# The output projection of an attention layer: prepared weights, one written order, and the seven products in another sequence

## The chip, the cores and the metric

The kernel runs on one core of a Trainium2 chip. A core has TensorE (PE: matmuls; PEld is its weight load), VectorE (DVE), ScalarE (ACT), GpSimd (POOL) and SyncE (SP), which here only issues DMAs. The engines run side by side, each through its own list of instructions in order. The metric is the device time of one execution in microseconds (us); lower is better.

## The reference

One model forward in float32 over 1024 latent tokens of width 1024 and 256 context tokens: an attention layer (windowed, 16 heads of 128), then a convolution layer (width 2048), each with a gate path, and a final norm. The part that the change touches is the end of the attention layer:

```
o = windowed_attention(q, k, v, kc, vc, sink)      # (1024, 2048)
y = (o * silu(z)) @ w_out                          # w_out: (2048, 1024)
x = x + gate * y
# then the next layer: rmsnorm(x), modulated, into the convolution's input projection
```

## The kernel before

**Precision.** Each matmul operand is held as a high part (rounded to the matmul's format, made by a copy on ACT) and a low part (the rest, made by a subtraction, `split_lo`, on DVE or POOL). A product takes three matmuls: high·high, high·low, low·high.

**Stages.** After a prologue, attention runs in 128 steps (8 pairs of heads, 16 blocks of 64 tokens): scores, softmax, transposes, values, with the input projection's matmuls filled in between. Then comes the output projection (`proj_attn`), then the convolution layer (`b_mm` for its input projection, then its own output projection).

**The output projection in seven products.** A = o·silu(z) is stored in DRAM, transposed, as `ozd`. It is cut in halves by tokens (h) and by its 2048 rows of K, W = `w_out` in halves by K and by columns (m), and the four quarters of the result are made with seven half-size products instead of eight. Two products, A11·W11 and A12·W21, are the steps with r = 0 of the list `SEQA` (eight steps); the other five have r = 1 to 5 and take sums of quarters. A step is 256 rows of K: four blocks b of 128 tokens, six matmuls of 512 columns each, so 24 matmuls. Steps 0 to 6 have their blocks 0 and 1 done inside attention (`EARLY_ROWS`), the remaining blocks follow after it.

**Weights prepared in attention.** The generator `low_parts` runs a little with each attention step. It makes the four sums of quarters of W that the products take (POOL, `minus`) and stores them in `wsums`, then the low parts of W's first 512 columns (`wolA`) and of the second layer's output weights (`wolC`). Each low part is one ACT copy and one POOL subtraction of 128x512 elements; `after` keeps them behind the softmax's operations of the same step. `store()` sends results out one step later.

**Operands of a step.** `load` fetches tiles of `ozd` and weights, `split` combines tiles on DVE and makes high and low parts; for r ≥ 1 the weights' low parts come from POOL. `ahead(nl, ns)` says up to which step loads and splits have been written. Loads go by SP's queue.

**Results.** Partial products are kept in SBUF (`m1`, `u2`, `u4`) and added on DVE from PSUM; `joined` multiplies such a partial result by the gate and adds it to the residual, on POOL; `evac0` then takes the last product from PSUM, multiplies by the gate, adds, stores x and squares it on ACT. It normalizes each 128-token block as soon as it is there (eight chains of norms of one column each). `turn_in` transposes normalized rows for the next layer (4 transposes a tile; DVE, ACT, then DVE or POOL); `bgA` places these tiles behind the steps, two at a time. The last three steps (`BYBLOCK`) are run block by block, not step by step.

**Order.** The program is written once for all engines. A planner reorders it by times that it models, except where `pin` keeps an engine in written order (`InOrder`, `keep_in_program_order`). From the end of the prologue only PE is pinned.

Of the kernel before, what the change touches and what calls it, by code (L numbers as in the profile page):

```python
# [40 lines left out]
LOAD_TO = {0: (8, 7), 1: (8, 7), 2: (9, 7), 4: (9, 8), 5: (10, 8), 6: (10, 8), 7: (11, 9)}  # L41
# [56 lines left out]
def backbone_kernel(  # L98
# [619 lines left out]
    wolA, wolC = (dr.tile([m, NK, P, 2, 512], F32, tag=n, name=n) for n, m in (("wolA", 1), ("wolC", 2)))  # L718
    wsums = dr.tile([4, NK // 2, P, 2, 512], F32, tag="wsums", name="wsums")
# [5 lines left out]
    made = []  # L725
# [8 lines left out]
    def low_parts():  # L734

        def raw(ap, name):
            t = pg.alloc(F32, [2, 512], name)
            SY.dma_start(out=t, in_=ap)
            return t

        def minus(a, b, at):
            after(tt(G, at, a, b, ALU.subtract), anchor_p)

        def pair(kt):
            return raw(Wo[kt * P:kt * P + P].rearrange("p (m n) -> p m n", m=2), "wb")

        def keep(t, which, kt):
            for m in range(2):
                made.append((wsums[which[m], kt // 2][:, kt % 2], t[:, m], t if m == 0 else None))

        u = pair(0)
        yield "open"
        for kt in range(KT):
            store()
            t = pair(kt + KT)
            minus(u[:, 1], u[:, 0], u[:, 0])
            yield "open"
            minus(t[:, 1], u[:, 1], u[:, 1])
            yield "open"
            minus(t[:, 1], u[:, 0], t[:, 1])  # L760
            keep(u, (0, 2), kt)
            yield "open"
            store()
            if kt + 1 < KT:
                u = pair(kt + 1)
            minus(t[:, 0], t[:, 1], t[:, 0])
            keep(t, (3, 1), kt)
            yield "shut"
        store()
        items = [(pair_rows(w, m, kk), d[m, kk]) for w, d, n in ((Wo, wolA, 1), (Wp, wolC, 2)) for m in range(n)  # L770
                 for kk in range(NK)]
        his = pg.alloc(F32R, [2, 512], "lhi")
        for src, dst in items:
            t = raw(src, "low")
            store()
            yield "open"
            for b in range(2):
                after(act(his[:, b], t[:, b], AF.Copy), anchor_a)
                after(split_lo(G, t[:, b], t[:, b], his[:, b]), anchor_p)
                if b == 0:  # L780
                    yield "open"
            made.append((dst, t, t))
            yield "shut"
        store()
        pg.free(his)
# [6 lines left out]
    def proj_attn():  # L792
# [14 lines left out]
        def load(i):  # L807
            r, kk = SEQA[i]
            if r == 0:
# [3 lines left out]
            k2 = kk + NK // 2  # L813
            rows = {1: ((1, kk), (1, k2), (0, kk)), 2: (), 3: ((0, k2),), 4: ((0, kk), (1, kk)), 5: ((1, k2),)}[r]
            st[i] = [o_raw(*a) for a in rows] + [w_raw(pair_rows(Wo, 1, k2) if r == 3 else
                                                       wsums[{1: 1, 2: 0, 4: 2, 5: 3}[r], kk])]
# [20 lines left out]
        def split(i):  # L837
# [3 lines left out]
            *rows, w = st[i]  # L841
            keep = False
            if r == 1:
                a21, a22, f = rows
                tt(V, a21, a21, a22, ALU.add)
                pg.free(a22)
                tt(V, f, a21, f, ALU.subtract)
                kept[(1, kk)], kept[(2, kk)] = a21, f
                keep = True
            elif r == 2:  # L850
                f = kept.pop((1, kk))
# [5 lines left out]
            elif r == 4:  # L857
                f, a21 = rows
                tt(V, f, f, a21, ALU.subtract)
                pg.free(a21)  # L860
            else:
                f, = rows
            oh, wh = pg.alloc(F32R, [2, 512], "ozh"), pg.alloc(F32R, [2, 512], "woh")
            act(wh, w, AF.Copy)
            act(oh, f, AF.Copy)
            wl, ol = pg.alloc(F32R, [2, 512], "wol"), pg.alloc(F32R, [2, 512], "ozl")
            for e in range(2):
                split_lo(G, wl[:, e], w[:, e], wh[:, e])
            split_lo(V, ol, f, oh)
            pg.free(w)  # L870
            if not keep:
# [25 lines left out]
        m1, u2, u4 = [], [], []  # L897

        def half_pages(ts, b, name):
            if b % 2 == 0:  # L900
                ts.append(pg.alloc(F32, [2, 512], name))
            return ts[b // 2][:, b % 2]
# [7 lines left out]
        for i in range(EARLY_ROWS):  # L910
            ahead(min(i + EA, EARLY_ROWS - 1), min(i + 1, EARLY_ROWS - 1))
            for b in range(2):
                yield from block(i, b, banks[4 + b])
                if i == 3:
                    act(half_pages(m1, b, "m1"), banks[4 + b], AF.Copy)
# [12 lines left out]
        def joined(us, xrs, m, keep=False):  # L928
            ns = slice(m * 512, m * 512 + 512)
            for b in range(4):  # L930
                u = us[b // 2][:, b % 2]
                g = hp.alloc(F32, None, "ug")
                tt(G, g[:, 0:512], u, gbc0[0][:, ns], ALU.mult)
                for xr in xrs:
                    t = xr[b // 2][:, b % 2]
                    tt(G, t, t, g[:, 0:512], ALU.add)
                hp.free(g)
                if b % 2 and not keep:
                    pg.free(us[b // 2])
# [3 lines left out]
        acc = [banks[b] for b in (4, 5, 0, 1)]  # L943
        for i, b in order:
            if b == 2 and i != 3:
                ahead(*LOAD_TO[i])
            if i == 4 and b == 2:
                xr = residual(0, 0)
            run(block(i, b, acc[b]))
            if i == 3:  # L950
                act(half_pages(m1, b, "m1"), acc[b], AF.Copy)
            if b == 3:
                done(i)
                bgA(0, i)
                if i == 4:
                    joined(m1, [xr], 0, True)
        for b in range(4):
            evac0(0, 0, b, acc[b], xr)
        held = []
        for i in range(8, len(SEQA)):  # L960
            r, kk = SEQA[i]
            acc = [banks[b] for b in ((2, 3, 4, 5) if r < 4 else (0, 1, 2, 3))]
            ahead(i + 3, i)
            if (r, kk) == (2, 2):
                xr12, xr22 = residual(0, 1), residual(1, 1)
            if (r, kk) == (3, 1):
                joined(u4, [xr12, xr22], 1)
            if (r, kk) == (4, 2):
                xr = residual(1, 0)
            if i >= len(SEQA) - BYBLOCK:  # L970
                ahead(i + 3, i + 1)
                held.append(i)
                bgA(r, kk)
                if kk == 3:
                    for b in range(4):
                        for n in held:
                            run(block(n, b, acc[b]))
                        evac0(1, 0, b, acc[b], xr)
# [3 lines left out]
            for b in range(4):  # L982
                run(block(i, b, acc[b]))
                if kk == 3 and r in (1, 2, 4):
                    with tc.high_priority():
                        d = {1: u2, 2: u4, 4: u2}[r]
                        d = half_pages(d, b, "u") if r < 4 else d[b // 2][:, b % 2]
                        tt(V, d, acc[b], (m1 if r == 1 else u2)[b // 2][:, b % 2], ALU.add)
                if b == 2:
                    ahead(i + 3, i + 1)  # L990
            done(i)
            bgA(r, kk)
            if kk == 3 and r > 2:
                for b in range(4):
                    evac0(r - 3, 1, b, acc[b], xr12 if r == 3 else xr22)
            if (r, kk) == (1, 3):
                pg.free(*m1)
            if (r, kk) == (4, 3):
                joined(u2, [xr], 0)
# [3 lines left out]
    def evac0(h, m, b, acc, xr):  # L1003
# [3 lines left out]
        if b % 2 == 0:  # L1007
            x1[(m, b // 2)] = pg.alloc(F32, [2, 512], "x1")
        if first:
            x1[b] = small([P, 2], name="ssf", bufs=8)  # L1010
        t, ss = x1[(m, b // 2)][:, b % 2], x1[b]
        tt(V, t, acc, gbc0[0][:, ns], ALU.mult)
        tt(G if b % 2 and h == 0 and first else V, t, t, xr[b // 2][:, b % 2], ALU.add)
# [4 lines left out]
        act(junk[:, 0:512], t, AF.Square, accum_out=ss[:, 1 - first:2 - first])  # L1018
        hp.free(junk)
        if first:  # L1020
            V.tensor_scalar(out=ss[:, 0:1], in0=ss[:, 0:1], scalar1=1.0 / D, scalar2=EPS, op0=ALU.mult, op1=ALU.add)
            return
        r = rstd_of(ss[:, 1:2], D, 1, ss[:, 0:1])
        for m in range(2):
            if b % 2 == 0:
                x1[("n", m, b // 2)] = pg.alloc(F32, [2, 512], "xn")
            d, f = x1[("n", m, b // 2)][:, b % 2], x1[(m, b // 2)][:, b % 2]
            if m:
                act(d, f, AF.Copy, scale=r)
            else:  # L1030
                V.tensor_scalar(out=d, in0=f, scalar1=r, scalar2=None, op0=ALU.mult)
            if b % 2:
                pg.free(x1[(m, b // 2)])
        if b == 3:
            h2pg[h] = []
            for kt in range(KT):
                later.append(lambda h=h, kt=kt: turn_in(h, kt))
# [420 lines left out]
    for i, (pr, st) in enumerate(steps):  # L1458
# [36 lines left out]
        if lstate[0] == "open" or i >= 5 and (h % 4 < 3 or qb < LOWS):  # L1495
            lstate[0] = next(lows, "shut")
        else:
# [541 lines left out]
    def bgA(r, kk):  # L2039
# [105 lines left out]
```

## Time and profile before

| | |
|---|---|
| median of 3 runs | 1703.49 us (1703.44 to 1707.1) |
| profiled execution | 1705.04 us, its span 1703.3 us |
| PE busy | 1657.2 us (97%) |
| DVE, ACT, POOL busy | 1155.3, 876.3, 1002.7 us |
| DMA | 248.85 MB, mean 146 GB/s |
| projection after attention | 805.3 to 989.4 us in the span |

The span runs from the first instruction to the last; the execution's own time is 1.7 us longer. In the profile, names are those of the program with numbers left out: `woh`, `wol` are high and low parts of weights, `wo` a loaded weight tile, `ozf` a loaded tile of `ozd`, `ozh`, `ozl` its parts, `m`, `u`, `x`, `xr`, `xn` partial results, output rows, residual and normalized rows, `hf`, `h2h`, `h2l` the next layer's input. `pss`, `psg`, `pso` are PSUM banks. Nearly all instructions carry line 92, a helper, so groups are told apart by tiles. A row "PE pss <- ACT m_page: 11.0, 2, 9.8" says that PE waited for ACT's work on that tile 11.0 us in total, 2 times, 9.8 us the longest.

### The profile page before, as it was taken

The page shows a single profiled execution, that of the slowest core. Times are in us where ns is not written, and L with a number is a line of the kernel's source. Part 1 is how long each engine was busy: PE and PEld are TensorE (multiplying, and loading weights), DVE is VectorE, ACT ScalarE, POOL GpSimd, SP SyncE. Part 2 cuts the span into 40 slices and gives each one's busy share as a digit, 9 for nine tenths or more (in the row PEclk, how much of TensorE's full clock was granted, in tenths as well). Part 3 has the DMA queues.
Part 4 walks back from the last instruction along what each step waited for, and adds up shares of the span by engine and source line. Part 5 has one row for each costly group of instructions (what it writes and reads, how often), then busy time and mean ns, then how long its engine had stood idle before and what let it go on. Part 6 is the DMA issues. An engine that isn't in the chain of part 4 may idle for free. (4 is left out here: it accounts for less than half of the span.)

```text
span 1703.3 us, 23865 instructions
## 1 busy us (share of the span) xinstructions
PE 1657.2 (97%) x8244; PEld 1385.0 (81%) x8244; DVE 1155.3 (68%) x2099; ACT 876.3 (51%) x1527; POOL 1002.7 (59%) x911
## 2 busy tenths in 40 slices
PE   9999999999999999999799699999999999999998
PEld 6888888888888888888577578888888888888886
DVE  5755554555355544565657979999999999867832
ACT  5644443555355544555343465655665665466731
POOL 0247673666547573742659857999898888130300
PEclk9999999999999999999799899999999999999999
DMA  9436553454335443467776222010121202377981
GB/s 383 162 94 191 171 167 112 140 167 126 104 116 175 133 143 91 144 229 257 258 236 204 99 81 100 13 63 25 49 75 38 93 32 80 124 260 246 326 285 51
DMA packets 142042, 248.85 MB, mean 146 GB/s; under 512 B 45034, under 2 KB 61730, under 8 KB 141920
## 3 DMA queue, kind: packets, MB, share of 16 engines
q1 hardware_dynamic: 135840, 237.35, 42.0%
q10 hardware_dynamic: 6080, 9.97, 2.4%
q8 instruction: 65, 1.06, 0.3%
q14 instruction: 57, 0.47, 0.1%
HBM read 190.90 MB, written 45.88 MB: 139 GB/s over the span
## 5 line engine op out<-in xcount | busy, mean ns | idle before, releaser
L92 POOL TENSOR_TENSOR odd_half<-odd_half,prod_half 128x513 f32<-128x513 f32 (+2 forms) x252 | 314.1, 1254 | 22.9 <-ACT prod_half L92 9.6
L92 POOL TENSOR_TENSOR wlo_page<-wraw_page,whi_page 128x512 fp32r<-128x512 f32 (+1 forms) x104 | 174.3, 1690 | 130.9 <-ACT whi_page L92 123.7
L92 PE MATMUL psg<-hh_page,whi_page 128*128 128x512 f32 x600 | 237.1, 395 | 0.0
L92 PE MATMUL psg<-hl_page,whi_page 128*128 128x512 f32 x600 | 235.0, 392 | 0.0
L92 PE MATMUL psg<-hh_page,wlo_page 128*128 128x512 f32 x600 | 234.5, 391 | 0.0
L92 ACT ACTIVATE prod_half<-ubuf,dww 128x513 f32<-128x513 f32 (+2 forms) x252 | 165.7, 675 | 116.8 <-POOL odd_half L92 113.1
L92 PE MATMUL psg<-h2h_page,whi_page 128*128 128x512 f32 x464 | 182.1, 392 | 0.0
L92 PE MATMUL psg<-h2h_page,wlo_page 128*128 128x512 f32 x464 | 180.9, 390 | 0.0
L92 PE MATMUL psg<-h2l_page,whi_page 128*128 128x512 f32 x464 | 180.8, 390 | 0.0
L92 DVE SCALAR_TENSOR_TENSOR pss<-ubuf,dww,pss 128x512 f32<-128x512 f32 (+3 forms) x270 | 172.7, 672 | 0.1
L92 DVE SCALAR_TENSOR_TENSOR pss<-ubuf,wsum,pss 128x512 f32<-128x512 f32 (+3 forms) x270 | 172.0, 672 | 0.2
L92 POOL TENSOR_SCALAR p_page<-p_page,sc 128x576 f32<-128x576 f32 (+2 forms) x128 | 93.2, 728 | 112.2 <-DVE sc L92 106.8
L92 ACT ACTIVATE pt<-pss 128x640 fp32r<-128x640 f32 (+1 forms) x128 | 86.6, 676 | 132.7 <-PE pss L92 132.5
L92 ACT ACTIVATE p_page<-p_page,sc 128x577 f32<-128x577 f32 (+2 forms) x128 | 96.9, 757 | 86.9 <-DVE sc L92 86.3
L92 DVE CUSTOM_DVE_ANT_0 p_page<-pss,mask_page,nsink 128x576 f32<-128x576 f32 (+1 forms) x112 | 90.2, 805 | 74.5 <-PE pss L92 48.5
L92 PEld LDWEIGHTS psg<-hh_page,wlo_page 128*128 128x128 f32 x600 | 112.8, 188 | 24.1
L92 PEld LDWEIGHTS psg<-hh_page,whi_page 128*128 128x128 f32 x600 | 112.8, 188 | 19.6 <-ACT hh_page L92 0.3
L92 PEld LDWEIGHTS psg<-hl_page,whi_page 128*128 128x128 f32 x600 | 113.2, 189 | 19.0 <-DVE hl_page L92 0.2
L92 DVE TENSOR_TENSOR pt<-pss,pt 128x640 fp32r<-128x640 f32 (+1 forms) x128 | 100.7, 787 | 32.2 <-ACT pt L92 32.1
L92 PE MATMUL pso<-h2h_page,wlo_page 128*128 128x512 f32 x304 | 118.4, 390 | 0.0
L92 PE MATMUL pso<-h2h_page,whi_page 128*128 128x512 f32 x304 | 118.4, 389 | 0.0
L92 PE MATMUL pso<-h2l_page,whi_page 128*128 128x512 f32 x304 | 118.4, 389 | 0.0
(273 smaller groups left out, 4060.4 us busy)
## 6 DMA issues: line engine op xcount, KB each, us to landing
wraw_page<-in_k_wconv_dram SPq DMA_DIRECT2D x48, 512.0 KB, 3.2
wraw_page<-in_k_win_dram SPq DMA_DIRECT2D x40, 512.0 KB, 4.0
ozf_page<-ozd SPq DMA_DIRECT2D x36, 512.0 KB, 5.5
wo_page<-in_conv_w_out_dram SPq DMA_DIRECT2D x32, 512.0 KB, 5.6
wol_page<-wolC SPq DMA_DIRECT2D x32, 512.0 KB, 5.6
rope_half<-rope_half ACTq DMA_DIRECT2D x76, 128.0 KB, 2.5
araw_page<-in_k_ada_dram SPq DMA_DIRECT2D x16, 512.0 KB, 10.0
dww_raw<-in_ada_w_dram SPq DMA_DIRECT2D x64, 128.0 KB, 2.7
```

Source lines behind the costliest of these rows:

```text
L92: r = f(*a, **k)
```

## The change

1. *Weights.* `low_parts` also makes the low parts of three of the four sums (`wslow`, 24 of 128x512) and of the lower half of W's second 512 columns (8 more in `wolA`): 32 more ACT copies and POOL subtractions in attention. High and low parts now go through half pages (`hp`, six of them, shared with the rotary embedding), and each half is stored at once. One more piece is run in twelve of the attention's steps, and loads pause near a change of head group.
2. *Order.* DVE, ACT and POOL are pinned beside PE for the rest of `proj_attn`, that is all of it after attention. SP's queue is left to the planner.
3. *Products.* S1·T1 comes before S2·T2 (S1 = A21 + A22, S2 = S1 − A11, T1, T2 sums of W). Fewer tiles of `ozd` are loaded (20 instead of 28 for r ≥ 1), three of the five products load low parts of sums and one those of a plain quarter, so POOL makes them only for r = 1. PSUM banks rotate over all six. Splits are written two steps ahead, loads three (`AHEAD`), with other values of `LOAD_TO` for the first product.
4. *Results.* `joined` is gone. DVE adds the kept partial sums to the last product (`first_sum`) as each block ends; gate, residual, store and squares (`evac0`) are written after the next step's loads and splits, from SBUF; the norm of a half is made once for its four blocks (`norm0`). `turn_in` tiles of the first half start one step earlier, behind r = 4, kk = 1.

```diff
-LOAD_TO = {0: (8, 7), 1: (8, 7), 2: (9, 7), 4: (9, 8), 5: (10, 8), 6: (10, 8), 7: (11, 9)}
+LOAD_TO = {4: (9, 7), 5: (9, 7), 6: (9, 8), 7: (10, 9)}
+AHEAD = (3, 2)
...
+        def low(t, b, d):
+            h = hp.alloc(F32R, None, "lhi")
+            hv = h[:, 0:512]
+            after(act(hv, t[:, b], AF.Copy), anchor_a)
+            after(split_lo(G, hv.bitcast(F32), t[:, b], hv), anchor_p)
+            SY.dma_start(out=d, in_=hv.bitcast(F32))
+            hp.free(h)
...
+            low(u, 1, wslow[2, kt // 2][:, kt % 2])
...
+            low(t, 1, wslow[1, kt // 2][:, kt % 2])
+            yield "open"
+            low(t, 0, wslow[3, kt // 2][:, kt % 2])
...
-            rows = {1: ((1, kk), (1, k2), (0, kk)), 2: (), 3: ((0, k2),), 4: ((0, kk), (1, kk)), 5: ((1, k2),)}[r]
...
+            rows = {1: ((1, kk), (1, k2)), 2: ((0, kk),), 3: ((0, k2),), 4: (), 5: ((1, k2),)}[r]
+            n = (0, 0, 1, None, 2, 3)[r]
+            st[i] = [[o_raw(*a) for a in rows], w_raw(pair_rows(Wo, 1, k2) if r == 3 else wsums[n, kk]),
+                     None if r == 1 else w_raw(wolA[1, k2] if r == 3 else wslow[n, kk], F32R)]
...
+                a21, f = rows
+                tt(V, f, a21, f, ALU.add)
+                kept[(1, kk)], kept[(3, kk)] = f, a21
             elif r == 2:
+                f, = rows
+                s1, a21 = kept.pop((1, kk)), kept[(3, kk)]
+                tt(V, a21, f, a21, ALU.subtract)
+                tt(V, f, s1, f, ALU.subtract)
...
+            acc = [banks[(2 + 4 * (r - 1) + b) % 6] for b in range(4)]
+            ahead(i + AHEAD[0], i + AHEAD[1])
+            while finish:
+                h, m, xr = finish.pop()
+                for b in range(4):
+                    evac0(h, m, b, xr)
+                norm0(h, m)
...
+                m, v = part("m", b), part("v", b)
+                if r == 1:
+                    tt(V, v, acc[b], m, ALU.add)
+                elif r == 2:
+                    tt(V, v, acc[b], v, ALU.add)
+                    tt(V, m, acc[b], m, ALU.add)
+                else:
+                    first_sum(r - 3, 1, b, acc[b], v)
+                    if r == 4:
+                        tt(V, m, acc[b], m, ALU.add)
...
+    def first_sum(h, m, b, acc, u):
+        if b % 2 == 0:
+            x1[(m, b // 2)] = pg.alloc(F32, [2, 512], "x1")
+        tt(V, x1[(m, b // 2)][:, b % 2], acc, u, ALU.add)
...
-        for _ in range(2 if r == 0 and kk or r == 4 and kk >= 2 or r == 5 and kk < 2 else 0):
+        for _ in range(2 if r == 0 and kk or r == 4 and kk or r == 5 and kk < 2 else 0):
...
+    pin("PVAG")
     run(projA)
+    pin("P")
```

More of the change, by code (lines that the diff above doesn't have):

```diff
@@ L914, in proj_attn @@
                 if i == 3:
[L915 removed]
+                    act(part("m", b), banks[4 + b], AF.Copy)
         yield "early"
@@ L954, in proj_attn @@
                 bgA(0, i)
[L955 to L958, printed above, removed]
         held = []
+        finish = [(0, 0, xr)]
         for i in range(8, len(SEQA)):
             r, kk = SEQA[i]
[L962 to L969, printed above, removed]
+            acc = [banks[(2 + 4 * (r - 1) + b) % 6] for b in range(4)]
[5 more added lines that the diff above has]
+                norm0(h, m)
+            if kk == 1 and r in (3, 4, 5):
+                xr = residual(*{3: (0, 1), 4: (1, 1), 5: (1, 0)}[r])
             if i >= len(SEQA) - BYBLOCK:
-                ahead(i + 3, i + 1)
                 held.append(i)
@@ L1006, in evac0 @@
         rows = slice((4 * h + b) * P, (4 * h + b + 1) * P)
[L1007 to L1013, printed above, removed]
+        if first and b == 0:
+            x1["ss"] = [small([P, 4], name="ssx4", bufs=2) for _ in range(2)]
+        t, ss = x1[(m, b // 2)][:, b % 2], x1["ss"]
+        tt(V, t, t, gbc0[0][:, ns], ALU.mult)
+        tt(V, t, t, xr[b // 2][:, b % 2], ALU.add)
         if b % 2:
```

179 lines of the change are left out of this document (85 added, 94 removed).

## The prediction

> **What bounds the kernel now.** I read the page first (span, PE row, clock row), then PE's waits, then stretches of the span with busy time by engine, then the timelines of PE, ACT and DVE where PE stands.
>
> ```profile
> span 1703.3 us, 23865 instructions
> PE   9999999999999999999799699999999999999998
> PEclk9999999999999999999799899999999999999999
> ```
>
> TensorE is busy almost throughout. The only dents, in its row and in its clock's, are slices 20, 22 and 23 (of 42.6 us each), the output projection. PE's waits over the whole span:
>
> ```profile
> PE pss L92 <- ACT m_page L92: 11.0, 2, 9.8
> PE pso L92 <- DVE ssf L92: 6.8, 1, 6.8
> PE pss L92 <- DVE u_page L92: 6.1, 4, 2.3
> PE pss L92 <- DVE x_page L92: 5.5, 3, 2.4
> PE pso L92 <- DVE xn_page L92: 3.3, 2, 2.7
> PE pss L92 <- POOL p_page L92: 2.0, 2, 1.8
> ```
>
> The first five, 32.7 us, are all of this stage. Its stretches (busy us of PE, PEld, DVE, ACT, POOL; clock; DMA share; GB/s) and, from the chain of waits, a run of 24 matmuls that waits for nothing:
>
> ```profile
> 130.00:765.00 635.00, 634.78 (x3498) 546.15 (x3497) 327.58 (x735) 303.82 (x648) 386.73 (x444) 1.00 0.49 147
> 805.30:989.40 184.10, 151.33 (x637) 120.99 (x636) 125.76 (x145) 69.76 (x101) 130.88 (x84) 0.91 0.59 194
> 820.00:830.00 10.00, 5.49 (x18) 4.10 (x19) 6.88 (x9) 1.54 (x2) 5.46 (x4) 0.50 0.92 320
> 960.00:970.00 10.00, 5.46 (x17) 4.63 (x18) 10.00 (x11) 4.96 (x8) 10.00 (x6) 0.52 0.37 131
> 1053.47 5.44 PE psg L92 x24
> ```
>
> A step (one entry of `SEQA`) is 24 matmuls, so 5.44 us, 0.227 us a matmul. Of the 28 × 24 = 672 matmuls, 84 run inside attention (seven steps, two blocks of six). The other 588 need 588 × 0.227 = 133.3 us; the 32 transposes of `turn_in` some 4 us and the 16 of the taps 1.3 us, by these rows:
>
> ```profile
> 950.35 1.03 PE L92 MATMUL pso<-ident,xn_page 128*128 128x128 f32 x8
> 811.08 0.68 PE L92 MATMUL pso<-ident,dwr_page 32*128 32x32 f32 x8
> ```
>
> So 138.6 us of work take 184.1 us: **45.5 us are lost**, 32.7 as waits, the rest (12.8) as matmuls at half clock behind them. That is the most that the change can win here. Why PE stood longest, from PE's and ACT's timelines:
>
> ```profile
> 824.51 0.79 PE L92 MATMUL pss<-woh_page,ozh_page 128*128 128x512 f32 x1 [9.81 <-ACT m_page L92]
> 825.10 0.63 PE L92 MATMUL pss<-wo_page,ozh_page 128*128 128x512 f32 x1
> 837.35 0.44 PE L92 MATMUL pss<-woh_page,ozl_page 128*128 128x512 f32 x1
> 892.57 0.50 PE L92 MATMUL pss<-woh_page,ozh_page 128*128 128x512 f32 x1 [2.30 <-DVE u_page L92]
> ...
> 814.07 1.06 ACT L92 ACTIVATE ozh_page<-ozf_page 128x1024 fp32r<-128x1024 f32 x1 [9.00 <-DMA ozf_page<-ozd]
> 822.92 1.06 ACT L92 ACTIVATE ozh_page<-ozf_page 128x1024 fp32r<-128x1024 f32 x1 [6.84 <-DVE ozf_page L92]
> 823.88 0.58 ACT L92 ACTIVATE m_page<-pss 128x512 f32<-128x512 f32 x1
> ```
>
> The planner had put the copy that empties PE's bank behind operand splits of later steps that waited for data. After that wait the clock is 0.50 and about 29 matmuls come 0.43 us apart instead of 0.227 (5.8 us lost); after 2.30 us it is not lowered.
>
> **The change part by part.** All in us; time from the trace of before.
>
> *Steps 0 to 7.* In written order ACT's two copies of the first product stand ahead of the splits of steps 7 and 8, so the 9.81 us wait and its slow clock go. Step 7's data had landed by 814.1 (ACT row above); PE reaches step 7 after 84 matmuls and the taps, at 805.3 + 19.0 + 1.3 = 825.6. Hence step 8 starts at 825.6 + 5.44 = 831.1. What hides the split of 7 is these 20 us; without the cover, 9 again.
>
> *Steps 8 to 19.* Bank rotation: each product starts on banks that the one before left longest ago, so the u_page waits (6.1) go. POOL loses the 32 weight splits of products 2 to 5 (they come as loads) and the 28 operations of `joined`. DVE gains 20 additions from PSUM. Durations, from groups by shape in this stage and DVE's timeline:
>
> ```profile
> L92 POOL TENSOR_TENSOR wol_page<-wo_page,woh_page 128x512 fp32r<-128x512 f32 x40 | 68.0, 1724 | 35.5 <-ACT woh_page L92 17.8 <-issue 8.1 <-DMA xr_page<-in_x_dram 4.1
> L92 DVE TENSOR_TENSOR ozl_page<-ozf_page,ozh_page 128x1024 fp32r<-128x1024 f32 x27 | 41.1, 1522 | 26.5 <-ACT ozh_page L92 18.7 <-POOL wol_page L92 3.7 <-issue 1.6
> L92 ACT ACTIVATE ozh_page<-ozf_page 128x1024 fp32r<-128x1024 f32 x27 | 28.5, 1054 | 65.9 <-DVE ozf_page L92 26.3 <-DMA ozf_page<-ozd 9.0 <-PE psg L92 8.5
> L92 DVE TENSOR_TENSOR u_page<-pss,u_page 128x512 f32<-128x512 f32 x6 | 4.1, 684 | 0.8 <-PE pss L92 0.8
> L92 DVE TENSOR_SCALAR hf_page<-pso,mod 128x512 f32<-128x512 f32 x8 | 6.4, 801 | 0.6 <-PE pso L92 0.6
> L92 ACT ACTIVATE h2h_page<-hf_page 128x512 fp32r<-128x512 f32 x8 | 5.1, 664 | 1.9 <-DVE hf_page L92 1.9
> L92 ACT ACTIVATE xn_page<-x_page,r 128x512 f32<-128x512 f32 x8 | 5.8, 721 | 9.6 <-DVE r L92 9.6
> L92 ACT ACT_TABLE_LOAD x2 | 2.6, 1283 | 0.0
> ...
> 872.40 1.23 DVE L92 TENSOR_TENSOR ozl_page<-ozf_page,ozh_page 128x1024 fp32r<-128x1024 f32 x1 [0.44 <-PE psg L92]
> 919.00 2.30 DVE L92 TENSOR_TENSOR ozl_page<-ozf_page,ozh_page 128x1024 fp32r<-128x1024 f32 x1 [3.68 <-POOL wol_page L92]
> 921.22 1.27 DVE L92 TENSOR_TENSOR x_page<-pss,gate_page 128x512 f32<-128x512 f32 x2
> 929.53 0.69 DVE L92 TENSOR_TENSOR x_page<-x_page,xr_page 128x512 f32<-128x512 f32 x1
> ```
>
> A 1024-wide DVE subtraction takes 1.23 where POOL rests and 2.30 beside a POOL subtraction; with POOL nearly empty I take 1.2 for it, and 0.6 for each of a row of 512-wide ones (two take 1.27). In written order one split is a chain on DVE: combine 1.2, wait for ACT's high part 1.05, low part 1.2, so 3.5 where one combination is made and 4.7 in product 2, where two are. That is less than 5.44 and two steps ahead. Added up in order from step 8's start: split of 10 done at 4.4, the eight additions and multiplications of `evac0` at 9.3, its sum of squares 10.4, splits of 11, 12, 13 at 14, 19, 24, product 1's four sums by 26, splits of 14, 15 at 31, 36. PE asks for 11 to 15 at 16.3, 21.8, 27.2, 32.6, 38.1. The margin is about 2 us, and POOL's eight remaining splits and late loads eat it. Bounds: 0, and 10 if each of the first five steps is 2 us late; I take 4, as the nearest rows for such a wait (u_page, 1.8 and 2.3) are two of them. Step 20 starts at 831.1 + 12 × 5.44 + 4 = 900.4.
>
> *Steps 20 to 27: where a new stall comes.* From step 20's start, DVE's written order is: last sum (0.7), low part of 22 (1.9), `evac0` (0,1), eight operations (6.7); then it stands for ACT's last square (7.5), table load and root (8.9), four small operations (9.7); the scaled rows on ACT (12.4), ACT's two high parts of 23 (14.3), low part (15.5). From there each step's pair of transposed tiles and its split run in turn on DVE and ACT: 0.80 + 0.66 + 0.68 + 0.80 + 0.66 + 0.95 + 1.05 + 1.2 = 6.8, against 5.44 + 1.0 of PE. Low parts of 24 and 25: 22.3 and 29.0. Product 4's eight additions: 33.8. Low part of 26: 40.5. `evac0` (1,1) and its squares: 46.2. Low part of 27: **52.9**. But steps 25 to 27 run block by block, so PE asks for 27 after 12 matmuls of them. It gets there at 41.9 (its own waits for banks and for 26 counted) and stands 11 us. That is long enough for the slow clock, by the row of 824.51: 5.8. The 60 matmuls that then remain: 13.6. End of the projection at 900.4 + 52.9 + 5.8 + 13.6 = 972.7, against 989.4. Bounds of this stretch (72.3): 47.5 with no wait (eight steps and the transposes), 80 if half of the DVE operations lie beside POOL's low parts.
>
> The Trainium skill ("TensorE: Matmul & The Clock Gate", Part 1) says that the clock halves after an idle window of about 3.4 us and returns after one busy window. By that rule the slow stretch would cost an estimated 1.7 us, not 5.8, and the end would come 4 us sooner. The trace shows 13 us of slow clock, from 824.5 to 837.4, and the trace decides.
>
> *After the last step.* `evac0` (1,0) and one four-wide norm now follow in one piece: 0.7 + 4.8 + 0.8 + 1.5 + 0.8 + 1.4 = 10 us. PE transposes these rows after two chunks and six matmuls, 10.9 + 1.4 = 12.3. Covered by 2 us; I take 1 (0 to 3, as ACT's first sigmoid queues behind).
>
> *Attention.* 32 more low parts: 32 ACT copies and 32 POOL subtractions, and 256 KB stores that stand in SP's queue until POOL is done; behind them queue the input weights' loads, which are asked for two chunks (some 20 us) ahead:
>
> ```profile
> L92 POOL TENSOR_TENSOR low_page<-low_page,lhi_page 128x512 f32<-128x512 f32 x48 | 62.3, 1298 | 45.4 <-ACT lhi_page L92 42.1 <-ACT p_page L92 3.0
> L92 ACT ACTIVATE lhi_page<-low_page 128x512 fp32r<-128x512 f32 x48 | 29.9, 624 | 0.0
> ```
>
> POOL +41.5 and ACT +20 over 635 us, from 387 and 304 busy: 67% and 51%. PE covers it (634.78 of 635.00) and waits for POOL's p_page 2.0 in all. I take +1, with −1 and +42 (all of POOL's) as ends. The stores' high parts now sit in the six half pages that rope uses; two allocations a step leave 17 us to each, so nothing.
>
> *Loads.* Per step 1.57 MB in products 1 to 3 (before: 2.1, 0.5, 1.0), 289 GB/s at full speed. The whole stage with its surroundings averaged less, with peaks above:
>
> ```profile
> DMA packets 23887, 47.21 MB, mean 203 GB/s; under 512 B 4874, under 2 KB 5259, under 8 KB 23873
> GB/s 406 407 365 43 185 140 275 274 67 280 334 191 405 355 208 233 221 147 261 268 283 300 38 90 186 358 180 138 321 277 81 0 90 81 12 290 118 45 70 111
> ```
>
> Bins of 5.8 us at 355 to 407 say that 289 can be had; it is in the 4 us above.
>
> **Sum.** 184.1 becomes 25.8 + 65.3 + 4 + 72.3 = 167.4: 16.7 won, less 1 and 1: 14.7. The profiled execution took 1705.04, 1.5 over the median of the runs; 1705.0 − 14.7 = 1690.3, on the median's scale **1689**.
>
> **Rivals.**
> 1. *The stage runs dry of waits* (5.44 a step): DVE's chain is shorter than added up, and step 27 is ready in time. For it: DVE's work without waits, about 110 us, is under 139. Against: the serial hand-over with ACT. Then the stretch of 72.3 takes its lower bound 47.5: 1689 − 25 = 1664. Chance 0.21.
> 2. *Loads become the bound* in steps 8 to 19, slower: if the queue gives only the 203 GB/s of the row above, a step takes 7.7, 12 × 2.3 = 27 more, less the 4 counted: 1689 + 23 = 1712. It decides below about 225 GB/s (7.0 a step, 18.7 in twelve, which is the 14.7 won and the 4 counted). Against: the 355 to 407. Chance 0.10.
> 3. *Attention pays* for its low parts: 1689 + 41 = 1730 in full; from 16 us on there is no gain. For it: POOL's p_page is already what PE waited for last. Chance 0.05.
> 4. *It does nothing that can be told*: the new stall gives back what the old ones cost; at the upper bound of the last stretch (+8) and with 8 instead of 4 in steps 8 to 19 the time is 1701. For it: steps 8 to 15 have a margin of only 2 us. Against: both ends at once. Chance 0.12.
>
> **Chances and range.** My forecast, 0.52, with its own range 1681 to 1697. A measurement of this kernel can't tell less than about 0.3% (5 us) from no change. Faster: 0.52 + 0.21 = 0.73; same: 0.12; slower, with rivals 2 and 3: 0.15. The range 1664 to 1704 takes in rivals 1 and 4 and leaves out the slower ones and a little below.
>
> **What would show it.** Right: no PE wait for m_page or u_page; clock 1.00 until step 24; POOL busy under 40 in the stage instead of 130.9; DVE's ozl near 1.25; one long PE wait for the operands of the last three steps, with a slow clock behind it; attention still 635 us of PE within 2. Wrong: PE waits spread over steps 8 to 19 with a DMA behind them (rival 2), PE waits on p_page or rope in attention (3), or none at all in the last three steps (1).

## The result, and the profile after

The changed kernel is slower by 0.9%: median 1720.4 us (four runs, 1720.0 to 1721.6) against 1705.3 (1703.4 to 1707.2) in the same comparison, a ratio of 1.009 with a 95% interval of 1.0072 to 1.0107. The prediction was 1689, with 0.73 on faster. From the page of the profiled execution after:

```profile
span 1718.9 us, 24011 instructions
PE   9999999999999999999878599999999999999998
PEclk9999999999999999999989699999999999999999
```

The dents of the projection are still there, and the deepest (slice 23, 5 in PE's row) is deeper than any before. PE's waits after (waited for; us in total, times, longest):

```profile
PE pss L93 <- DVE part_page L93: 20.0, 4, 9.8
PE pss L93 <- ACT ozh_page L93: 10.0, 1, 10.0
PE pss L93 <- DVE x_page L93: 5.9, 4, 3.5
PE pss L93 <- POOL p_page L93: 4.4, 4, 1.4
...
PE pss L93 <- ACT part_page L93: 1.4, 2, 0.7
```

The long wait for ScalarE's copies (`m_page`, 11.0, now `part_page`) is down to 1.4, as forecast, and one wait of 10.0 for the operands of step 27 has come, as forecast. Not forecast: 20.0 for VectorE's `part_page`, the sums that took over from `u_page` (6.1 before).

Now by stretches: attention; steps 0 to 7; 8 to 19; 20 to 27; the rest. The borders are starts of steps, counted off in PE's timeline at 24 matmuls a step. Columns as in the prediction. After:

```profile
130.00:765.00 635.00, 631.98 (x3480) 542.83 (x3479) 324.43 (x729) 316.68 (x675) 426.12 (x473) 1.00 0.53 162
807.50:840.80 33.30, 28.42 (x126) 22.07 (x125) 11.28 (x15) 8.05 (x9) 9.20 (x14) 0.95 0.85 297
840.80:921.10 80.30, 69.26 (x289) 55.84 (x288) 47.97 (x51) 27.71 (x33) 2.67 (x2) 0.93 0.64 222
921.10:999.40 78.30, 54.51 (x225) 42.43 (x224) 40.41 (x58) 28.32 (x44) 9.79 (x6) 0.83 0.45 148
999.40:1718.90 719.50, 708.70 (x3160) 586.11 (x3158) 610.16 (x1011) 411.09 (x613) 444.08 (x327) 0.99 0.33 115
```

The same borders before:

```profile
805.30:848.50 43.20, 32.19 (x126) 24.88 (x125) 23.75 (x23) 10.76 (x12) 22.87 (x22) 0.76 0.79 265
848.50:918.50 70.00, 65.88 (x289) 53.95 (x289) 38.30 (x34) 24.63 (x30) 52.57 (x31) 1.00 0.69 222
918.50:989.50 71.00, 53.36 (x225) 42.23 (x225) 63.82 (x89) 34.37 (x60) 55.54 (x33) 0.90 0.36 123
989.50:1703.30 713.80, 706.22 (x3160) 585.43 (x3158) 599.64 (x1005) 403.62 (x601) 440.71 (x325) 1.00 0.33 115
```

| stretch | before | predicted | after | after − before | after − predicted |
|---|---|---|---|---|---|
| attention's end | 805.3 | 806.3 | 807.5 | +2.2 | +1.2 |
| steps 0 to 7 | 43.2 | 25.8 | 33.3 | −9.9 | +7.5 |
| steps 8 to 19 | 70.0 | 69.3 | 80.3 | +10.3 | +11.0 |
| steps 20 to 27 | 71.0 | 72.3 | 78.3 | +7.3 | +6.0 |
| the rest | 713.8 | 714.8 | 719.5 | +5.7 | +4.7 |
| span | 1703.3 | 1688.5 | 1718.9 | +15.6 | +30.4 |

So the gain of steps 0 to 7 was won in part and given back more than twice over. Where steps 8 to 19 lost it, PE's timeline after at step 11, first block to third (the first row of slow matmuls and the first at full clock behind it):

```profile
858.47 0.39 PE L93 MATMUL pss<-woh_page,ozl_page 128*128 128x512 f32 x1
866.35 0.80 PE L93 MATMUL pss<-woh_page,ozh_page 128*128 128x512 f32 x1 [7.49 <-DVE part_page L93]
...
871.99 0.39 PE L93 MATMUL psg<-wol_page,ozh_page 128*128 128x512 f32 x1
```

and VectorE's timeline over the same time:

```profile
859.65 1.23 DVE L93 TENSOR_TENSOR ozl_page<-ozf_page,ozh_page 128x1024 fp32r<-128x1024 f32 x1 [1.12 <-ACT ozh_page L93]
860.79 2.48 DVE L93 TENSOR_TENSOR ozf_page<-ozf_page,ozf_page 128x1024 f32<-128x1024 f32 x2
864.47 1.22 DVE L93 TENSOR_TENSOR ozl_page<-ozf_page,ozh_page 128x1024 fp32r<-128x1024 f32 x1 [1.20 <-ACT ozh_page L93]
865.62 0.68 DVE L93 TENSOR_TENSOR part_page<-pss,part_page 128x512 f32<-128x512 f32 x1
```

PE stops in the middle of a step whose operands are all there: the first block of step 11 is done, and the second, which accumulates in another bank, starts only when VectorE has read the first one's bank. In the program the two banks are the two halves of one tile (`ps_s`, 1024 words), and the instruction list has a wait for VectorE at just this matmul: it writes words 512 to 1023 of the tile, and the semaphore value that it waits for is reached by the sum that reads words 0 to 511. The sum stands behind the split of step 13, and that split is a chain with ScalarE. The Trainium skill ("PSUM — Partial Sum Buffer", "PSUM bank collisions raise a hardware error") says that accesses of two engines to different banks run clean. By that the wait is the program's and not the chip's; no run here lets a read and a matmul lie in the two halves at once.

### The profile page after: what moved, and what is told of

It reads as the page before. It is cut to its first block, busy times and chain, and to the rows that moved or that the text cites. A ratio compares the mean times of both kernels' runs of the same rounds, so it can differ in the third digit from the quotient of the medians.

```text
span 1718.9 us, 24011 instructions
## 1 busy us (share of the span) xinstructions
PE 1661.1 (97%) x8244; PEld 1384.5 (81%) x8244; DVE 1139.1 (66%) x2085; ACT 891.8 (52%) x1555; POOL 934.2 (54%) x881
## 5 line engine op out<-in xcount | busy, mean ns | idle before, releaser
L93 POOL TENSOR_TENSOR wlo_page<-wraw_page,whi_page 128x512 fp32r<-128x512 f32 (+1 forms) x104 | 174.0, 1690 | 135.6 <-ACT whi_page L93 113.1
L93 ACT ACTIVATE pt<-pss 128x640 fp32r<-128x640 f32 (+1 forms) x128 | 86.6, 677 | 144.0 <-PE pss L93 138.6
```

The source lines that it names most:

```text
L93: r = f(*a, **k)
```

## The experiments

Two theories were set against each other first. *H (halves)*: the wait is for the other half of the tile, and written order makes it long. *L (late operands)*: VectorE's chain of splits is late in any case, and what PE doesn't wait at a sum it will wait at the next step.

| | order of DVE, ACT, POOL in the stage | PE waits for the other half in a product's last step | median us | ratio to before (95%) |
|---|---|---|---|---|
| changed kernel | written | yes | 1720.4 | 1.0072 to 1.0107 |
| experiment 1 | written | no | 1699.9 | 0.9942 to 0.9973 |
| experiment 2 | planner | yes | 1705.9 | 0.9986 to 1.0005 |
| experiment 7 | planner | no | 1685.9 | 0.9875 to 0.9904 |

The third column is about VectorE's sums. ScalarE's two copies behind the first product hold the other half as well: 7.7 and 7.9 us in the planner's order, 1.4 in written order.

**1. Reads after blocks.**

```diff
             for b in range(4):
                 run(block(i, b, acc[b]))
-                if kk < 3:
-                    continue
+            for b in range(4 if kk == 3 else 0):
                 m, v = part("m", b), part("v", b)
...
-            if i == 7:
-                first_sum(0, 0, b, acc[b], part("m", b))
+            if i == 7 and b == 3:
+                for j in range(4):
+                    first_sum(0, 0, j, acc[j], part("m", j))
...
-            acc = [banks[(2 + 4 * (r - 1) + b) % 6] for b in range(4)]
+            acc = [banks[(2 + 4 * (r - 1) + b) % 6 if r < 5 else (0, 2, 1, 3)[b]] for b in range(4)]
```

> The changed kernel, only in the last step of each product the VectorE sums are written behind all four blocks of matmuls instead of behind each block, and the three held steps use their four banks in the order 0, 2, 1, 3 instead of 0, 1, 2, 3. Theory H (halves): two neighbouring banks are one tile of the program, so a block's first matmul waits until the sum of the block before it has read the other half; in written order that sum stands behind an operand split, and PE waits for VectorE though its own bank is free. It expects the waits for part_page (20.0) and x_page (5.9) to fall under 4 together, the stage to be 16 to 25 us shorter, one wait of 8 to 16 us left at the split of step 27, and a median of 1696 to 1705 where the changed kernel has 1720. Rival L (late operands): VectorE's chain of splits is late anyway, and what PE doesn't wait at a sum it waits at the next step's operands; it expects waits for ozh_page or ozl_page in place of those for part_page, and 1714 or more.

Measured: 1699.9, with 20.6 us won by moving a few VectorE instructions by some lines and naming the held steps' banks in another order. Its stretches:

```profile
809.70:837.80 28.10, 26.73 (x125) 21.12 (x124) 11.59 (x14) 8.06 (x9) 9.15 (x14) 1.00 0.91 309
837.80:907.10 69.30, 67.23 (x290) 55.16 (x289) 47.42 (x51) 27.73 (x33) 3.75 (x3) 0.98 0.79 274
907.10:979.00 71.90, 53.33 (x225) 41.70 (x224) 40.71 (x59) 28.61 (x44) 9.96 (x6) 0.88 0.49 162
```

and its waits:

```profile
PE pss L93 <- ACT ozh_page L93: 10.6, 1, 10.6
PE pss L93 <- DVE part_page L93: 6.3, 2, 4.2
```

`x_page` is out of the list; `part_page` keeps 6.3, where 4 for both was expected: the next product now reaches a bank whose own sum is still late, by 2.1 us at the third block of step 12 and by 4.2 at the second of step 24. The stage takes 169.3 us where the prediction had 167.4: steps 8 to 19 are 69.3, the very number predicted. That it is the very number is in part luck: the prediction took 4 for two short waits at a full clock, and here one wait of 2.1 and the slow clock behind it make up the 4. So H holds, and with this wait gone the prediction's sum for these steps comes out.

**2. The planner's order.** `pin("PVAG")` becomes `pin("P")`, nothing else.

> The changed kernel, with VectorE, ScalarE and GpSimd left to the planner's order in this stage; TensorE in written order as in both kernels. Products, banks, loads and low parts as changed. Theory H expects the long waits for part_page to go, since the planner can put a sum ahead of a split that is not due, and the wait for the split of step 27 to shrink: 1694 to 1704. Rival L, or one by which the product order or the loads cost the time, expects 1714 or more.

Measured: 1705.9, 14.6 less than the changed kernel; 2 us above the expected range. The waits for the halves didn't go, they moved:

```profile
PE pss L93 <- DVE x_page L93: 10.9, 4, 4.6
PE pss L93 <- ACT part_page L93: 7.7, 2, 7.0
PE pss L93 <- DVE part_page L93: 7.1, 4, 2.9
```

The expectation was right for steps 11 and 23, where the waits are shorter (2.95 and 1.38 instead of 7.49 and 9.78), and wrong that the planner cures the halves: in step 7 the wait is longer (4.62 instead of 3.51), at the second held block it is 3.87, and the wait for ScalarE's copies is back (7.0). What it does cure is step 27 (no wait for `ozh_page` over 0.4).

**3. The kernel before in written order.** `pin("PVAG")` ahead of the projection in the kernel before, nothing else.

> The kernel before, with nothing but VectorE, ScalarE, GpSimd and TensorE in written order in the output projection. Theory H expects written order by itself to cost: sums of a product's last step behind splits, 1712 to 1730 against 1705, with waits for u_page or x_page above 15 us together, though the wait for m_page (9.8) goes. The rival that written order helps (what the prediction assumed) expects 1690 to 1702.

Measured: 1748.1 (1.0245, 1.023 to 1.026), 41 us slower and far above the range. The sign is H's, the cause mostly not: `x_page` and `u_page` together are 13.2, under the 15 expected, and most of the loss is elsewhere.

```profile
PE pss L92 <- ACT ozh_page L92: 26.5, 4, 10.3
PE pss L92 <- POOL wol_page L92: 16.6, 4, 15.0
PE pss L92 <- DVE x_page L92: 8.9, 5, 5.8
...
PE pss L92 <- DVE u_page L92: 4.3, 4, 1.9
```

In written order POOL's weight splits stand behind the twelve operations of `joined`, and operands stand behind residuals, norms and transposed tiles. So written order alone is a loss, also without any of the change's own parts; the 41 us hold for this program, which left these engines' order to the planner.

**4. Split of step 27 early.** `ahead(i + AHEAD[0], i + AHEAD[1] + (i == 24))`, nothing else.

> The changed kernel, only the split of step 27 is written before step 24 (right behind the split of 26), ahead of the eight operations of evac0 (1,1) and two pairs of transposed tiles. Theory C (the written chain on VectorE and ScalarE makes step 27 late) expects the wait for ozh_page of 10.0 to fall under 2 and the slow clock behind it to go: 10 to 15 us earlier at the end of the projection, 1705 to 1711. A rival: the chain only moves to the end, where TensorE then waits for xn_page by as much: 1716 or more. The waits for part_page stay as they are in both.

Measured: 1719.5 (1.0062 to 1.0108): no gain. The wait for `ozh_page` is gone as expected, and a longer one stands in its place, at the second of the held blocks:

```profile
982.16 0.80 PE L93 MATMUL pss<-woh_page,ozh_page 128*128 128x512 f32 x1 [12.71 <-DVE x_page L93]
```

Neither theory had named this: the operands were ready, but the sum of the first held block stood behind `evac0` (1,1), two transposed tiles and two weight splits, and the second block lies in the other half. That is H again, at a place where the late split had covered it.

**5. The other half asked for later.** No instruction is moved; products 1 and 4 use banks 2, 4, 3, 5.

```diff
-            acc = [banks[(2 + 4 * (r - 1) + b) % 6] for b in range(4)]
+            acc = [banks[(2, 4, 3, 5)[b] if r in (1, 4) else (2 + 4 * (r - 1) + b) % 6] for b in range(4)]
```

> The changed kernel, no instruction moved: the second and fourth product only use their banks in the order 2, 4, 3, 5 instead of 2, 3, 4, 5, so that the half of the tile whose sum is late is asked for one block later. Theory H expects the waits of 7.5 and 9.8 us in steps 11 and 23 to move from the second block (behind 6 matmuls) to the third (behind 12) and to be 1.4 us (six matmuls at 0.227) shorter each; a median 2 to 5 us under the changed kernel. If the sum itself or the operands of the step were what PE waits for (rival L), the waits stay at the second block, as long as they were.

Measured, in one run: 1718.3, which is too little to tell 2 us by; the places of the waits tell more. PE's timeline at steps 11 and 23:

```profile
860.65 0.39 PE L93 MATMUL psg<-woh_page,ozl_page 128*128 128x512 f32 x1
866.16 0.80 PE L93 MATMUL pss<-woh_page,ozh_page 128*128 128x512 f32 x1 [5.13 <-DVE part_page L93]
...
949.95 0.79 PE L93 MATMUL pss<-woh_page,ozh_page 128*128 128x512 f32 x1 [8.42 <-DVE part_page L93]
```

The second block (`psg`) now runs without a stop, and the wait stands at the third. In step 11 it is 2.4 us shorter (7.49 to 5.13), in step 23 1.4 (9.78 to 8.42, the expected amount). With the same sums at the same places in VectorE's list, only the names of the banks decide where PE stops: this is the plainest proof of H. The other 1.0 us of step 11 is no effect of the names: PE comes to the step 0.8 later (858.15 instead of 857.34) and the sum 0.2 earlier (865.42 instead of 865.62).

**6. Experiments 1 and 4 together.**

> Reads after blocks (the first experiment) and the split of step 27 written before step 24 (the fourth) together. Theory H with C: in the fourth experiment the split was ready but a sum behind evac0 (1,1) then held the other half of the tile for 12.7 us; with both, neither is left. Expected: no wait above 5 us in the stage after step 24, the end of the projection 10 to 16 us before that of the first experiment, 1684 to 1692. If the chain on VectorE and ScalarE is too long whatever its order, a wait of 8 us or more comes back at the held steps or at xn_page behind the projection, and the median stays at 1696 or more.

Measured: 1695.2 (0.9928 to 0.9958), between the two expectations: 4.7 us less than experiment 1, not 10 to 16. A wait of 8.70 for `x_page` is left at the third held block, which shares a tile with the first. VectorE's list has the sum of the first held block behind `evac0` (1,1), two transposed tiles and two weight splits, so here the length of the written chain, L's cause, decides how late the other half comes free. Both theories hold, each in its part.

**7. Experiments 1 and 2 together.**

> Reads after blocks with VectorE, ScalarE and GpSimd in the planner's order (the first two experiments together). The planner's order alone left 10.9 (x_page) + 7.7 + 7.1 (part_page) of waits. Theory H expects the x_page and VectorE part_page waits, 18 us with the slow clock of two of them (6), to go: 1682 to 1692 against 1706. If these waits were the planner's due times and not the halves, 1700 or more.

Measured: 1685.9, inside H's range. Waits for `x_page` and VectorE's `part_page` are no longer in the list; what is left is ScalarE's copies and step 27:

```profile
PE pss L93 <- ACT part_page L93: 7.9, 2, 7.2
...
PE pss L93 <- ACT ozh_page L93: 3.9, 1, 3.9
PE pss L93 <- DVE ozl_page L93: 3.6, 1, 3.6
```

The table above is now full, and the two causes add: the other half costs 20.6 us in written order and 19.9 in the planner's; written order costs 14.6 with that wait and 13.9 without it. The medians come from three comparisons, in which the kernel before took 1704.8 to 1707.0; by the ratios it is 22.7 and 18.1, and 16.2 and 11.6, so they add to within some 5 us.

**8. The same edit in the kernel before** (sums behind the blocks, banks 2 and 3 for the second half of the first product, 2, 0, 3, 1 for the last).

> The kernel before, with nothing but the same edit of banks and reads: steps 4 to 7 accumulate their last two blocks in banks 2 and 3 rather than in the banks that the copies of step 3 still read, the sums of a product's last step stand behind its four blocks, the last product's banks go 2, 0, 3, 1. Theory H expects the waits for m_page (11.0) and u_page (6.1) and part of x_page (5.5) to go with the slow clock behind the first (5.8): 1682 to 1692 against 1705. The prediction's reading (bank reused too soon by the next product, late reads) expects at most the m_page part: 1690 to 1705.

Measured: 1695.2 (0.9928 to 0.9961), a gain of 9.5 where H expected 13 to 23. By its time alone it lies in the range of the prediction's reading (1690 to 1705), so only the places of the waits can tell. `u_page` falls from 6.1 to 2.6, and none of its four waits of before is left; the 2.6 is a new one, at the first block of step 16, whose own bank the late sums now still hold:

```profile
889.59 0.47 PE L92 MATMUL pss<-woh_page,ozh_page 128*128 128x512 f32 x1 [2.62 <-DVE u_page L92]
```

`m_page` stays at 8.2: the copy of step 3's third block was left ahead of step 2's fourth block, which lies in the other half; the new banks had missed that place. The second of its waits (1.2 before, at step 4's third block) is gone with the new banks, and 15 slow matmuls follow the first instead of 29. And in the held steps 8.7 for `hf_page` stand where 6.8 for `ssf` stood before.

**9 to 12. Towards a faster kernel.** Experiment 9 is 7 with that place put right too:

```diff
+            if i == 4:
+                acc = [banks[n] for n in (4, 5, 2, 3)]
...
-            if i == 3:
-                act(part("m", b), acc[b], AF.Copy)
+            if i == 3 and b == 3:
+                for j in (2, 3):
+                    act(part("m", j), acc[j], AF.Copy)
```

(banks 0, 1 and 2, 3 change places in the steps behind it). Experiment 10 adds experiment 4's line. Experiment 11 is 7 with written order kept up to step 7, 12 is 11 with experiment 4's line.

> Reads after blocks in the planner's order, as in the experiment before, and also the first product's two late copies (its last two blocks, step 3): they stand behind both blocks, and steps 4 to 7 accumulate in banks 2 and 3, so that no matmul waits for ScalarE's copies until step 8; the later products' banks are swapped to fit. Left over before it: 7.2 + 0.7 for part_page (ScalarE) with a slow clock, and 3.9 + 3.6 at step 27. Theory H expects the 7.9 and its slow clock (2 to 4) to go: 1674 to 1679. If the planner then puts the copies so late that step 8 waits for them, or the time is given back at step 27, 1682 or more.

> The same, and the split of step 27 asked for before step 24. Expected: of the waits at step 27 (3.9 + 3.6 and a slow clock) 4 to 8 us less: 1667 to 1675. If VectorE's and ScalarE's chain through the transposed rows is the limit there, as the held steps showed in written order (8.7 us at x_page), the same as without it within 3 us.

> Reads after blocks; VectorE, ScalarE and GpSimd in written order up to step 7 and in the planner's order from step 8. Banks as in the changed kernel. This tells written order's good side (ScalarE's copies ahead of later splits, 0.7 + 0.7 instead of 7.2 + 0.7) from its bad one: 1676 to 1681. If written order costs as much in steps 0 to 7 as it wins there, 1685 or more.

> The same with the split of step 27 asked for before step 24: 4 to 8 us less than without it, 1669 to 1676; within 3 us of it if the chain is the limit.

Measured: 1679.3 (9), **1669.0** (10), 1687.8 (11), 1676.7 (12); the ratios' intervals are 0.9832 to 0.9864, 0.9768 to 0.9797, 0.9881 to 0.9916 and 0.9816 to 0.9845. Experiment 9 ends 0.3 us above what H expected, experiment 12 0.7 above its range. Experiment 11 goes to its rival: with written order up to step 7 ScalarE's copies cost 1.4, but the four sums of step 7 make PE wait 6.8 at the third block of step 8, in a bank that one of them still holds. Early splitting is worth 10.3 (10) and 11.1 us (12), more than the 4 to 8 expected, once the sums hold little up and the planner orders these steps, against 0.9 in experiment 4 and 4.7 in experiment 6. Experiment 10 beats both kernels, by 2.2% over the one before. Its stretches:

```profile
810.60:839.50 28.90, 26.54 (x128) 21.49 (x127) 15.71 (x16) 10.07 (x11) 11.59 (x16) 1.00 0.88 309
839.50:905.50 66.00, 65.61 (x290) 54.01 (x289) 46.76 (x56) 27.30 (x33) 1.24 (x1) 1.00 0.83 300
905.50:954.00 48.50, 47.45 (x225) 38.99 (x224) 39.37 (x61) 27.74 (x46) 13.02 (x5) 1.00 0.66 229
954.00:1668.10 714.10, 706.24 (x3160) 585.09 (x3158) 605.66 (x1006) 407.08 (x607) 448.69 (x328) 1.00 0.33 115
```

The clock is 1.00 all through, and 143.4 us for the stage are 4.8 more than the 138.6 of matmuls and transposes that the prediction counted. VectorE's list there shows how:

```profile
934.43 1.53 DVE L93 TENSOR_SCALAR hf_page<-pso,mod 128x512 f32<-128x512 f32 x2
935.87 1.22 DVE L93 TENSOR_TENSOR ozl_page<-ozf_page,ozh_page 128x1024 fp32r<-128x1024 f32 x1
937.00 0.69 DVE L93 TENSOR_TENSOR x_page<-x_page,gate_page 128x512 f32<-128x512 f32 x1
```

While ScalarE makes the high part of a tile, VectorE does a split or a residual, where in the changed kernel it stood 2.6 to 2.7 us at each split of steps 24 to 27; that of step 25 there:

```profile
949.65 1.23 DVE L93 TENSOR_TENSOR ozl_page<-ozf_page,ozh_page 128x1024 fp32r<-128x1024 f32 x1 [2.62 <-ACT ozh_page L93]
```

## Why the prediction was wrong

*Steps 0 to 7.* Right: the 9.81 us for `m_page` went, because the copy came early. But the cause had been read wrongly. What the prediction calls "the copy that empties PE's bank" empties the bank beside it: 36 matmuls lie between 805.55 and the stop, so PE stood at step 2's fourth block, whose bank was free, and the instruction list has it wait for the copy of the third block, the other half of that tile. The largest wait before was already the wait that the change then ran into elsewhere. Wrong by 7.5 us (step 8 at 840.8, not 831.1): 5.2 for the other half in step 7 with its slow clock (33.3 against 28.1 in experiment 1, where it is gone), and 2.3 for two waits of 0.7 for the copies and for starts and small transposes that were counted too short.

*Steps 8 to 19: the step that failed.* "Bank rotation: each product starts on banks that the one before left longest ago, so the u_page waits (6.1) go", with 4 us taken. The waits for `u_page` weren't a product on a bank that is still being read; they were a block waiting for the other half of its own tile. In the changed kernel experiment 5 shows it. Before, all four stand at the second or fourth block of a product's last step, and the instruction list has each wait for the sum that reads the other half; in step 11, from PE's and VectorE's timelines:

```profile
868.21 0.50 PE L92 MATMUL pss<-woh_page,ozh_page 128*128 128x512 f32 x1 [1.82 <-DVE u_page L92]
867.48 0.68 DVE L92 TENSOR_TENSOR u_page<-pss,m_page 128x512 f32<-128x512 f32 x1
```

Rotation between products doesn't touch that, and written order lengthens it. The prediction's own list had the number: it put product 1's sums behind the split of 13, at 24 to 26 us from the start of step 8, and the first of them came at 24.8 (865.62 − 840.8). It asked when PE needs step 12 and not what in step 11 waits for the sum. Waits and slow clock took 80.3 − 65.3 = 15.0 us where 4 were taken and 10 was the upper bound; step 11 alone has 7.49 and some 2.7 of slow clock. With that one cause gone, experiment 1 shows the 69.3 forecast, in part by luck, as said there.

*Steps 20 to 27.* Right that a stall comes at the split of step 27, and nearly right in its size: 11 was forecast, and 10.0 + 1.7 came. The sum fits better than its parts. The slow clock behind it cost about 3 us (14 slow matmuls), not 5.8. In experiment 1 PE comes to step 27 after 43.2 us (41.9 forecast) and stands 10.6 + 1.7, and the stretch takes 71.9 where 72.3 was forecast; in the changed kernel it takes 78.3, and the 9.8 of step 23 are the same failed step once more. And the late split was only one of two causes of this stall: with it early, experiment 4 stands 12.71 for the other half. That the written hand-over between VectorE and ScalarE makes the split late, as the prediction argued, fits the runs: an early split alone leaves 8.70 in written order (experiment 6), the planner's order alone 4.6 + 3.9 (experiment 9), and both together end the stall (experiment 10). The first rival (47.5 for this stretch) was thus possible, but not with this order: experiment 10 takes 48.5.

*After the last step.* 1 taken (0 to 3), 4.7 more came. The chain was reckoned at 10 us with VectorE at 0.7 an operation; it took 15:

```profile
1001.73 2.90 DVE L93 TENSOR_TENSOR x_page<-x_page,gate_page 128x512 f32<-128x512 f32 x1
1004.66 2.77 DVE L93 TENSOR_TENSOR x_page<-x_page,xr_page 128x512 f32<-128x512 f32 x1
```

Two operations lay beside POOL's low parts of the next layer's weights (5.55 us for two, from 1001.34 on POOL). The prediction had used the same effect for the splits (1.23 against 2.30) and not here. The Trainium skill ("SBUF — State Buffer", "Who interferes with whom") says that such an instruction with two operands in SBUF contends with a POOL instruction that reads SBUF, for a port pair that is locked exclusively; 2.90 instead of 0.69 beside POOL instructions of 2.8 agrees. The four runs in the planner's order that were read for it (2, 7, 9, 10) spend 714 to 715.5 us behind the projection, the changed kernel's runs in written order (1, 4, 5, 6 and itself) 719.3 to 719.6. It isn't written order as such: the kernel before, which normalizes each block by itself, spends 713.6 in it (experiment 3). Nor is the contention absent from experiment 10, where two of the last operations take 2.19 and 2.77; but there only the last block's two operations stand behind the last sum, in the changed kernel all eight.

*Attention.* 1 taken, 2.2 came: PE's waits for `p_page` went from 2.0 to 4.4, POOL from 386.73 to 426.12 busy in the 635 us (41.5 forecast, 39.4 came).

*The sign.* The rivals on the other side were loads and attention. Neither decided: experiment 10 loads some 278 GB/s over the stage (its three rows by their lengths) at full clock. The two costs that did decide weren't among the rivals: the other half of the tile, and written order, which was taken as a gain throughout; experiment 2 prices it at 14.6 us in the changed kernel, experiment 3 at 41 in the kernel before. Of the prediction's own signs, POOL fell as forecast (21.7 us in the stage), while the clock didn't stay at 1.00 until step 24 (0.95 and 0.93 up to step 19).

*A reading.* The rows of before have their dents in slices 20 and 23; slice 22, which the prediction also named, shows 9 in both. Nothing in its sum hangs on it.

## What to carry to other kernels

When an order is written out by hand, ask of every read of PSUM what stands ahead of it on its engine, and what stands behind it on PE: here the answer was a block of the same tile. Two banks in one tile of the program are one thing to its waits; put consecutive blocks in different tiles, or write the reads behind all of them. And try a removed wait together with its neighbour: the early split was worth 0.9 us alone, 4.7 with the sums out of the way, and 10 with the planner's order as well.

## What the runs showed of the hardware

The slow clock was sized wrongly. The prediction took 5.8 us from one stretch (29 matmuls) and set the Trainium skill's rule aside ("TensorE: Matmul & The Clock Gate", Part 1: an idle window of about 3.4 us halves the clock, one busy window restores it). After the 7.49 us wait 13 matmuls came at 0.43 (866.35 to 871.99), which costs 5.64 − 13 × 0.227 = 2.7 us: more than the 1.7 by the rule, less than half of 5.8. The row of 13 us before had small transposes and a second stop of 1.20 us in it; that these kept the clock down was only argued. Experiment 8 keeps the eight small transposes there, without the second stop, and its slow stretch lasts 7.9 us (822.26 to 830.11, behind a wait of 8.23). And a stop of 2.07 us (experiment 1, step 12) was enough for a slow stretch, which began a microsecond after it and lasted 3.4 us:

```profile
865.60:869.00 3.40, 3.40 (x10) 2.66 (x9) 2.43 (x3) 0.85 (x1) 0.00 (x0) 0.51 0.19 72
869.00:879.00 10.00, 10.00 (x46) 8.25 (x45) 7.28 (x7) 5.19 (x6) 0.00 (x0) 1.00 0.80 265
```

whereas 2.30 us in the kernel before left the clock at full. So a wait's length alone doesn't tell: waits of 2 to 3 us do it at times (2.37 in experiment 8 did, 2.62 there didn't), while of the waits of 3.5 us and more that were looked at each did.
